# A transformer block on one core: a written order for its first input tiles, and the edges of its attention

## The chip, the cores and the metric

The kernel runs on one core of a Trainium2 chip. The metric is the device time of one execution in microseconds (us). The time of the kernel before is 2206.74 us, the median of three runs (2206.45 to 2209.09).

A core has a matrix engine (TensorE, PE in the profile, with PEld for its weight loads), a vector engine (VectorE, DVE), a scalar engine (ScalarE, ACT), GpSimd (POOL) and a sync engine (SP) that issues most DMA transfers. The engines run side by side, each takes its own instructions in order, and semaphores hold them to one another. Matrix products are written to PSUM, which has eight banks of 128x512 f32; SBUF is the working memory.

## The reference, cut to what matters

One block of a diffusion transformer for 512 latent tokens and 256 context tokens, width 2048, in float32:

```python
mod_l = (silu(c) @ w_ada + b_ada)[:, None, :]          # six vectors of 2048
mod_c = (silu(c_ctx) @ w_ada + b_ada)[None, None, :]
h_l = modulate(rms_norm(x, g_mix_norm), sh_a, sc_a)
h_c = modulate(rms_norm(ctx, g_mix_norm), csh_a, csc_a)
qa_l, kva_l, kr_l, cb_l, cc_l, ch_l = split_projection(h_l @ w_in)
qa_c, kva_c, kr_c, ... = split_projection(h_c @ w_in)
k_l, v_l = mla_key_value(kva_l, kr_l, g_kv_a, w_kv_b, rope_lat)
k_c, v_c = mla_key_value(kva_c, kr_c, g_kv_a, w_kv_b, None)
q_l = mla_query(qa_l, g_q_a, w_q_b, rope_lat)           # rms_norm(q_a, g_q_a) @ w_q_b
att_l = block_attention(q_l, [k_l, k_c], [v_l, v_c])    # softmax(q k * 192**-0.5) v, 8 heads
conv_l = short_conv(cb_l, cc_l, ch_l, conv_w, conv_b)
x = x + gt_a * merge_heads(att_l, conv_l, g_mix_out, w_out)
hf_l = modulate(rms_norm(x, g_ffn_norm), sh_f, sc_f)
x = x + gt_f * conv_ffn(hf_l, w_up, ffn_conv_w, ffn_conv_b, w_down)   # 2 x 5504 wide
return rms_norm(x, g_final)
```

## The kernel before

Activations lie transposed: a tile is 128 channels by 512 tokens, and x is 16 such tiles. Every product is made in three passes: both operands are split into a rounded part (hi, type fp32r, a cast on ScalarE) and the rest (lo, a subtraction on VectorE), and `mm3` (lines 169 to 172) multiplies hi by hi, hi by lo and lo by hi into one PSUM bank. `split` and `blocks` (145 to 164) do this for weights, `hilo` (297) for activations. Instructions are put in order by a planner that simulates the program on a timeline; `keep` holds an instruction in the order in which it is written, and `tc.issue_after(ins)` puts the instructions of its block behind `ins` on the same engine.

The stages in order of time:

- **Front** (lines 405 to 416). `silu_rows` loads c, spreads it over the partitions with a product by ones and takes its SiLU into `sv`. The 16 tiles of x are loaded; `add_squares` squares each on ScalarE and adds the squares on VectorE into one running sum. Then `silu_rows` does the same with c_ctx (tile `cc`, into `svc`), the table of small vectors `sm` is loaded, and `rms` sums the squares over the partitions (products with a column of ones, L283), takes the root and the reciprocal (`rsqrt`, 261 and 262) and spreads the result over the partitions (`spread`, L267) into `rl`.
- **Input projection** (524 to 569). Its 16 input tiles are taken in three chunks (`KCH = [2, 4, 10]`), and within a chunk over 31 column tiles of 128, the first six of them row by row (`pf`), the others one by one (`pp`); `evac` copies or adds the bank into `acc`. `prep(j)` makes input tile j: two rows of w_ada of 1 MB each (t = 16 + j and j) are loaded as two halves and multiplied with `sv` on VectorE with a running sum (`dot_v`, L216), and `modulate` (395) scales x by `rl` (398), by scale and shift (401) and splits it. `todo` (518) says after which column which tile is made. `ctx_mods` (481) does the same dots for the context with `svc` (L491) in the third chunk.
- **Attention** (576 to 801). `ctx_tile` projects the context. The loop (772) has 32 steps, eight heads by four blocks of 128 query rows. `softmax` (678) takes the maximum of a row of scores (L683), multiplies it by -SCALE (L684) and takes the exponential (L687); `transposes` (690) turns p by six transposes (L700) and splits it; `attend` multiplies by the values (`po`). `pieces` makes the next pair of heads' q, k and v in the same steps, `fetch` loads their weights. `merge_sum` (718) sums the squares of a pair of heads and raises them to -1/2 on GpSimd (L732); `merge` (735) spreads that by products with the identity (L741). `gn_apply` does the same for the convolution's groups. Meanwhile the later rows of w_ada (t = 32 to 79) are loaded whole (`ada_raw`, tile `ra`) into the same two `raw` buffers as the weights, and multiplied by `late_dot` (L238).
- **Output projection** (886 to 906). Six columns row by row over 16 rows (`of`), eight columns one by one (`whole`, `o`), and the last two in two halves of 256 tokens (`ol`); `residual` adds to x, and squares for the next norm are summed.
- **Upward projection** (1000 to 1122). The first six columns row by row (`uf`), the others, in pairs f, by a scheme of seven products of half matrices; `acts` (933) makes convolution, SiLU and gate of a pair. `first_acts` (1092) holds the three pairs that come from the first six columns.
- **Downward projection** (1173 to 1226) in three groups of columns, and the last norm.

PSUM is handed out from two pools until line 1038: four tiles of one bank (`sml`) and two of two banks (`big`), which `bank` and `first_banks` deal out in turn. The norm's sums, the scores of a step and the pair `ol` are `big` tiles. From line 1039 on there are eight tiles of one bank, in the cyclic order of `BANKS` (36).

SP's queue takes the loads of x, w_in and w_ada in written order up to line 548 (`ordered`).

## Time and profile before

| | |
|---|---|
| median of three runs | 2206.74 us (2206.45 to 2209.09) |
| the profiled execution, its own time | 2206.8 us |
| its span, first to last instruction | 2204.9 us, 34542 instructions |
| mean granted TensorE clock | 0.996 |
| read from HBM, written | 442.73 MB, 20.71 MB |
| DMA queue of SP (hardware_dynamic, q1) | 405.03 MB, 54.1% of 16 engines' span |
| chain of work that ended last, by engine | TensorE 91%, VectorE 4%, DMA 2%, ScalarE 2% |

The profile records one execution. Its times differ from the runs' by the 1.9 us that lie around the span. Busy shares are means over stages with different limits, so the stages have to be read one by one; a row of the table of stages gives the length of a stretch and, for each engine, its busy time and (in brackets) its instructions, then the granted clock of TensorE as a share of full speed, the busy share of the DMA engines and what they moved. In a line of a group stand the code line, engine and operation, what it writes and reads, the shape and count, then the busy time and the mean length of one in ns, and the idle time of the engine just before these instructions with what ended it. Matmuls are pipelined, so a record of one is longer than its distance to the next.

### The profile page before, as it was taken

The page shows a single profiled execution, that of the slowest core. Times are in us where ns is not written, and L with a number is a line of the kernel's source. Part 1 is how long each engine was busy: PE and PEld are TensorE (multiplying, and loading weights), DVE is VectorE, ACT ScalarE, POOL GpSimd, SP SyncE. Part 2 cuts the span into 40 slices and gives each one's busy share as a digit, 9 for nine tenths or more (in the row PEclk, how much of TensorE's full clock was granted, in tenths as well). Part 3 has the DMA queues.
Part 4 walks back from the last instruction along what each step waited for, and adds up shares of the span by engine and source line. Part 5 has one row for each costly group of instructions (what it writes and reads, how often), then busy time and mean ns, then how long its engine had stood idle before and what let it go on. Part 6 is the DMA issues. An engine that isn't in the chain of part 4 may idle for free.

```text
span 2204.9 us, 34542 instructions
## 1 busy us (share of the span) xinstructions
PE 2149.2 (97%) x13346; PEld 1914.2 (87%) x13346; DVE 1599.0 (73%) x2493; ACT 1010.5 (46%) x1635; POOL 111.3 (5%) x149
## 2 busy tenths in 40 slices
PE   7899999999999999999999999999999999999998
PEld 4688888878888888899999999999999888888887
DVE  7998887678896848777777777777777873633544
ACT  5523333544452237555554555555554432532444
POOL 0000000000000000011111011111110000000000
PEclk9999999999999999999999999999999999999999
DMA  8989884434469925577777777777776995753462
GB/s 331 344 276 334 275 279 150 144 120 149 158 235 358 331 86 172 132 196 201 204 194 195 201 205 195 194 201 201 201 193 200 350 345 159 247 164 92 160 210 88
DMA packets 144264, 466.75 MB, mean 212 GB/s; under 512 B 16290, under 2 KB 20642, under 8 KB 138082
## 3 DMA queue, kind: packets, MB, share of 16 engines
q1 hardware_dynamic: 125652, 405.03, 54.1%
q0 software_dynamic: 16272, 57.42, 12.8%
q8 instruction: 104, 1.70, 0.3%
q10 hardware_dynamic: 2176, 2.10, 0.3%
q14 instruction: 60, 0.49, 0.1%
HBM read 442.73 MB, written 20.71 MB: 210 GB/s over the span
## 4 chain that ended last, share of the span: by engine, by line
PE 91%; DVE 4%; DMA 2%; ACT 2%; issue 1%; SPq 0%; POOL 0%; DVEq 0%; ACTq 0%
PE d L170 7%; PE d L172 7%; PE d L171 7%; PE pp L170 4%; PE pp L172 4%; PE pp L171 4%; PE o L172 1%; PE o L171 1%; PE o L170 1%; PE uf L170 1%; PE uf L171 1%; PE uf L172 1%; PE of L172 1%; PE pf L171 1%; PE of L170 1%; PE of L171 1%
## 5 line engine op out<-in xcount | busy, mean ns | idle before, releaser
L997 POOL DMA_DIRECT2D u_s<-in_w_up x80 | 68.1, 851 | 416.3 <-DMA u_s<-in_w_up 353.4
L153 ACT CAST w_0h<-rw 128x512 fp32r<-128x512 f32 (+1 forms) x63 | 38.5, 618 | 107.3 <-PE pp L171 65.7
L216 DVE SCALAR_TENSOR_TENSOR ada<-ada,sv 128x1024 f32<-128x1024 f32 x64 | 77.4, 1217 | 4.6 <-DMA ada<-in_w_ada 4.6
L491 DVE SCALAR_TENSOR_TENSOR ada<-ada,svc 128x1024 f32<-128x1024 f32 x64 | 75.9, 1218 | 2.0 <-DMA ada<-in_w_ada 1.8
L238 DVE SCALAR_TENSOR_TENSOR ra<-ra,sv 128x1024 f32<-128x1024 f32 x50 | 59.4, 1216 | 0.0
L154 DVE TENSOR_TENSOR w_0l<-rw,w_0h 128x512 fp32r<-128x512 f32 (+1 forms) x63 | 42.4, 680 | 21.8 <-ACT w_0h L153 21.8
L238 DVE SCALAR_TENSOR_TENSOR ada<-ada,sv 128x1024 f32<-128x1024 f32 x46 | 55.7, 1218 | 2.6 <-DMA ada<-in_w_ada 2.6
L1108 DVE TENSOR_TENSOR u<-u,u 128x1024 f32<-128x1024 f32 x40 | 49.0, 1225 | 1.3
L1107 DVE TENSOR_TENSOR u<-u,u_s 128x1024 f32<-128x1024 f32 x40 | 48.7, 1217 | 0.0
L939 POOL DMA_DIRECT2D y_d<-a x43 | 24.7, 576 | 386.2 <-DVE a L938 376.7
L732 POOL TENSOR_TENSOR gr<-gr,half 128x8 f32<-128x8 f32 x4 | 8.3, 2084 | 641.4 <-DVE mx L684 505.3
L238 DVE SCALAR_TENSOR_TENSOR adl<-adl,sv 128x1024 f32<-128x1024 f32 x32 | 38.8, 1218 | 0.2 <-DMA adl<-in_w_ada 0.2
L683 DVE TENSOR_REDUCE mx<-s 128x1 f32<-128x768 f32 x32 | 30.4, 951 | 8.4 <-PE s L673 8.4
L704 DVE TENSOR_TENSOR ptl<-t,pth 128x384 fp32r<-128x384 f32 x64 | 33.2, 548 | 4.2 <-ACT pth L703 4.2
L502 DVE TENSOR_TENSOR acc<-acc,pp 128x512 f32<-128x512 f32 x50 | 33.9, 678 | 1.9 <-PE pp L172 1.8
L703 ACT CAST pth<-t 128x384 fp32r<-128x384 f32 x64 | 28.5, 488 | 14.3 <-PE t L700 14.1
L936 ACT ACTIVATE g<-g 128x512 f32<-128x512 f32 x43 | 27.2, 633 | 12.1 <-DVE g L930 12.1
L928 ACT ACTIVATE g<-cg,sm 128x512 f32<-128x512 f32 x40 | 32.5, 813 | 0.0
L687 ACT ACTIVATE p<-s,mx 128x768 f32<-128x768 f32 x32 | 29.3, 915 | 6.8 <-DVE mx L684 6.6
L928 ACT ACTIVATE a<-ca,sm 128x512 f32<-128x512 f32 x40 | 32.1, 802 | 0.0
L700 PE MATMUL t<-io,p 128*128 128x128 f32 x192 | 27.5, 274 | 3.7 <-ACT p L687 2.4
L929 DVE SCALAR_TENSOR_TENSOR g<-cg,sm,g 128x511 f32<-128x511 f32 x40 | 29.8, 745 | 0.0
(15580 smaller groups left out, 8734.8 us busy)
## 6 DMA issues: line engine op xcount, KB each, us to landing
ada<-in_w_ada SPq DMA_DIRECT2D x174, 512.0 KB, 6.0
u<-in_w_up SPq DMA_DIRECT2D x120, 512.0 KB, 8.3
u_s<-in_w_up SPq DMA_DIRECT2D x80, 512.0 KB, 4.1
u_s<-in_w_up POOLq DMA_DIRECT2D x80, 512.0 KB, 9.5
d<-in_w_dn SPq DMA_DIRECT2D x86, 384.0 KB, 3.8
y<-y_d SPq DMA_DIRECT2D x129, 256.0 KB, 4.5
ra<-in_w_ada SPq DMA_DIRECT2D x25, 1024.0 KB, 4.8
adl<-in_w_ada SPq DMA_DIRECT2D x32, 512.0 KB, 6.0
```

The costliest lines, as they stand in the source:

```text
L153: A.copy(out=hi[:, :n], in_=raw[:, a:a + n])
L154: V.tensor_tensor(out=lo[:, :n], in0=raw[:, a:a + n], in1=hi[:, :n].bitcast(F32), op=ALU.subtract)
L170: PE.matmul(ps, w[0], x[0], start=first, stop=False, skip_group_check=on_top)
L171: PE.matmul(ps, w[0], x[1], start=False, stop=False, skip_group_check=on_top)
L172: PE.matmul(ps, w[1], x[0], start=False, stop=last, skip_group_check=on_top)
L216: V.scalar_tensor_tensor(out=r, in0=r, scalar=1.0, in1=vec[:, i * 1024:(i + 1) * 1024], op0=ALU.mult, op1=ALU.mult, accum_out=col[:, i:i + 1])
L238: keep(V.scalar_tensor_tensor(out=r, in0=r, scalar=1.0, in1=svs[i], op0=ALU.mult, op1=ALU.mult, accum_out=lc[:, t % 4:t % 4 + 1] if i else ...
L491: keep(V.scalar_tensor_tensor(out=raw[q], in0=raw[q], scalar=1.0, in1=svc[:, q * 1024:(q + 1) * 1024], op0=ALU.mult, op1=ALU.mult, accum_o ...
L928: A.activation(u, src, AF.Identity, bias=s("fb", m), scale=s("fw", 86 + m))
L997: G_.dma_start(r[-1], src[more], accum_op=ALU.add)
L1107: V.tensor_tensor(out=a11, in0=a11, in1=s1, op=ALU.add)
L1108: V.tensor_tensor(out=a12, in0=a12, in1=a11, op=ALU.add)
```

## The change

It has several parts.

1. **Front.** `sm` is loaded ahead of x. The order of ScalarE and VectorE is written out (`pinned`, `pin`) from the start to the second input tile. The squares are added up in groups of five, each group is summed on TensorE when it is complete, and the last tile of x is a group of its own. The rows t = 16, 0, 17 and 1 of w_ada are loaded and multiplied in quarters (`ada_quarters`, `dot_quarter`), and weights of the first two tiles are split at written places (`low`). After that the casts of weights are held behind the second tile's cast (`gate`) until the eighth column of the first chunk. c_ctx is no longer loaded here: at the second chunk one DMA spreads it over the partitions and one activation takes its SiLU.
2. **Spreading.** `spread` and `merge` transpose a broadcast column instead of multiplying it by the identity.
3. **Attention.** -SCALE is folded into `g_q`; `softmax` takes the minimum, and the exponential has scale -1. `q_nope(1, 0)` is made ahead of the loop, `merge` comes one step later, weights are fetched and late tiles loaded at other steps, the last four `gn_apply` run inside the loop, and the exponential's table is asked for early.
4. **End of attention.** The eight single banks begin here. Four of the 16 rows of the output projection's first six columns (`OUT_EARLY`) stand ahead of `merge(3)`.
5. **Banks.** `ol`, the norm's sums and `uf` are single banks, and `BANKS` has another order.
6. **First activations.** One of the three pairs is taken in the middle of the first turn, one at its end, one at the end of the next.

The diff, cut to its core:

```diff
-BANKS = [0, 1, 7, 4, 5, 6, 2, 3]
+BANKS = [7, 6, 2, 3, 4, 5, 1, 0]
+OUT_EARLY = 4
...
+    def pin(ins):
+        if pinned[0]:
+            keep(ins)
+        return ins
...
-        A.copy(out=hi[:, :n], in_=raw[:, a:a + n])
-        V.tensor_tensor(out=lo[:, :n], in0=raw[:, a:a + n], in1=hi[:, :n].bitcast(F32), op=ALU.subtract)
+        with tc.issue_after(gate[0]) if gate else ExitStack():
+            pin(A.copy(out=hi[:, :n], in_=raw[:, a:a + n]))
+        if not pinned[0]:
+            V.tensor_tensor(out=lo[:, :n], in0=raw[:, a:a + n], in1=hi[:, :n].bitcast(F32), op=ALU.subtract)
+            return hi, lo
+        lows.append((lo, hi, raw, a, n))
...
     def spread(pb, r):
         for g in range(r.shape[1]):
-            PE.matmul(pb[:, g * P:(g + 1) * P], bc(r[:, g:g + 1], P), ident, start=True, stop=True)
+            PE.transpose(pb[:, g * P:(g + 1) * P], bc(r[:, g:g + 1], P), ident)
...
+        def dot_quarter(t):
+            q, col = quarters[t]
+            i = 4 - len(q)
+            r = q.pop(0)
+            pin(V.scalar_tensor_tensor(out=r, in0=r, scalar=1.0, in1=sv[:, i * T:(i + 1) * T], op0=ALU.mult, op1=ALU.mult, accum_out=col[:, i:i + 1]))
+            if i == 3:
+                pin(V.tensor_tensor(out=col[:, :2], in0=col[:, :2], in1=col[:, 2:], op=ALU.add))
+                total(col, t, mod[:, t:t + 1])
...
-        silu_rows(c, sv, "c")
...
-        silu_rows(c_ctx, svc, "cc")
-        fetch_to(sm, small)
-        rms([ssq], D, T, rl)
+        pinned[0] = True
+        A.activation(tiny(1, "silu"), eps, AF.Silu)
+        silus = silu_rows(c, sv, "c")
+        next(silus)
+        fetch_to(sm, small)
+        xs = []
+        def squares():
+            for j in range(NK):
+                xs.append(t2([P, T], F32, f"xr{j}"))
+                fetch_to(xs[j], xt[:, j * T:(j + 1) * T])
+                if j == NK - 1:
+                    quarters[16] = ada_quarters(16)
+                ssq = add_squares(ssq if j % 5 else None, xs[j], T, f"xs{j}")
+                if j in (1, 3, 5):
+                    next(silus)
+                if j == NK - 1:
+                    dot_quarter(16)
+                    dot_quarter(16)
+                if j % 5 == 4 or j == NK - 1:
+                    yield ssq
+        quarters = {}
+        rms(squares(), D, T, rl, 4)
+        dot_quarter(16)
+        dot_quarter(16)
+        first_raw = load(w_in[:, :2 * G * P], 2 * G * P, "rf00")
+        quarters[0] = ada_quarters(0)
+        quarters[17] = ada_quarters(17)
+        quarters[1] = ada_quarters(1)
+        first_w = blocks(first_raw, 8, "wf00")
+        normed(0)
+        for _ in range(4):
+            dot_quarter(0)
+        modulate(0, 2)
+        first_w += blocks(first_raw, 4, "wf08", 8)
+        low()
+        for t in (17, 1):
+            for _ in range(4):
+                dot_quarter(t)
+        normed(1)
+        modulate(1)
+        pinned[0] = False
+        gate.append(last_hi[0])
...
+                fetch_to(svc, c_ctx.to_broadcast([P, D]))
+                A.activation(svc, svc, AF.Silu)
...
-            mx = tiny(1, f"mx{hd}{tt}")
-            V.tensor_reduce(mx, ss[:, :768], axis=AX.X, op=ALU.max)
-            V.tensor_scalar(mx, mx, scalar1=-SCALE, scalar2=None, op0=ALU.mult)
+            mn = tiny(1, f"mn{hd}{tt}")
+            V.tensor_reduce(mn, ss[:, :768], axis=AX.X, op=ALU.min)
...
+        fetch(1, 0)
+        late_load(ada_raw)
         for f, i in ((k_ctx, 0), (k_ctx, 1), (values, 2)):
             f(0, i)
...
+        q_nope(1, 0)
+        fetch(1, 1)
...
-            elif n % 8 == 1 and n > 1:
+            if n % 8 == 2 and n > 8:
                 merge(n // 8 - 1)
             late_dot(1)
-            if n % 4 != 3:
+            if n > 24 and n % 2:
+                deque(late_bg[4 + (n - 25) // 2], 0)
+            at = n % 8
+            if at == 0 and n and n < 24:
+                fetch(pr + 1, 1)
+            if pr < 3 and n:
+                f, p_, i = pieces(pr + 1)[at]
+                f(p_, i)
+            if at < 2 and n < 24:
+                fetch(pr + 1, 2 + at)
+            elif at >= 2 and n < 29:
                 late_load(ada_raw)
+                if at == 6 and n < 16:
+                    fetch(pr + 2, 0)
+            if n in (29, 30):
+                k = 2 * (n - 29)
+                out_raw[k] = load(w_out_first[k // 2], 2 * G * P, f"ofr{k}")
             pump(2)
+        ph_ps.close()
+        p8 = ctx.enter_context(tc.tile_pool(name="p8", bufs=1, space=PSUM, reuse_waits="tile"))
...
         merge_sum(3)
-        for g in late_bg[4:]:
-            deque(g, 0)
+        pss = [bank_of(g, f"of{g}") for g in range(G)]
+        mix = []
+        for k in range(OUT_EARLY):
+            if k % 2 == 0:
+                w = row_weights(w_out_first, k, "of", raw=out_raw[k])
+            out_row(k, w)
         merge(3)
...
-    b = big("ol")
-    pso = [b[:, :512], b[:, 512:]]
+    pso = [sml("ol0"), sml("ol1")]
...
-    pss = first_banks("uf")
+    pss = [bank_of(i, f"uf{g}") for g, i in enumerate((2, 3, 4, 5, 1, 0))]
...
-        while first_acts:
+        if first_acts and f == G // 2:
             acts(*first_acts.pop(0))
```

More of the change, by code (lines that the diff above doesn't have):

```diff
@@ L389, in mods, with normed @@
             ada(j)
+        def normed(j):
+            keep(V.tensor_tensor(out=xs[j], in0=xs[j], in1=rl, op=ALU.mult))
         def prep(j):
@@ L573, in block_kernel, with half_of, row, row_weights @@
         del spare["w"]
+    HS = [slice(0, T // 2), slice(T // 2, T)]
+    def half_of(w, h):
+        return tuple(z[:, HS[h]] for z in w)
+    def row(pss, w, x, k, cols=slice(0, T)):
+        for g in range(G):
+            mm3(pss[g][:, cols], w[g], tuple(z[:, cols] for z in x), k == 0 and cols.start == 0, k == NK - 1)
+    def row_weights(src, k, nm, held=False, raw=None):
+        raw = load(src[k // 2], 2 * G * P, f"{nm}r{k}") if raw is None else raw
+        if held:
+            r = []
+            for b in range(0, 2 * G, 4):
+                w = hilo(raw[:, b * P:(b + 4) * P], 4 * P, f"{nm}w{k}_{b}")
+                r += [part(w, q) for q in range(4)]
+        else:
+            r = blocks(raw, 2 * G, f"{nm}w{k}")
+        return r[:G], r[G:]
     mixa = [None] * NH
@@ L739, in merge @@
                 pb_ = sml(f"gb{hd}")
-                for g in range(4):
-                    PE.matmul(pb_[:, g * P:(g + 1) * P], bc(r[:, i * 4 + g:i * 4 + g + 1], P), ident, start=True, stop=True)
+                spread(pb_, r[:, 4 * i:4 * i + 4])
                 o = oo[hd]
@@ L1036, in block_kernel @@
         t_sums(j)
-    ph_ps.close()
-    p8 = ctx.enter_context(tc.tile_pool(name="p8", bufs=1, space=PSUM, reuse_waits="tile"))
-    banks = deque(BANKS)
-    def bank_of(i, nm):
-        return p8.tile([P, 512], F32, tag=f"s{i}", bufs=1, name=nm)
-    def bank8(nm):
-        banks.rotate(-1)
-        return bank_of(banks[-1], nm)
-    for i in range(8):
-        bank_of(i, f"bank{i}")
+    bank8 = in_turn(BANKS)
     one_bank[0] = bank8
```

138 lines of the change are left out of this document (73 added, 65 removed).

## The prediction

> **What bounds the kernel now.** I read the busy line first, then a table of the engines' busy time by stage, then TensorE's waits over the whole run, its waits inside the attention loop, and last the chain of waits up to the first real product.
>
> ```profile
> PE 2149.2 (97%) x13346; PEld 1914.2 (87%) x13346; DVE 1599.0 (73%) x2493; ACT 1010.5 (46%) x1635; POOL 111.3 (5%) x149
> ```
>
> TensorE is occupied for 97% of the span, so no edit can win more than what lies in its gaps, in stages where it only looks busy, and in products that are not needed. The table of stages (length, then PE, PEld, DVE, ACT and POOL busy, granted clock, DMA share, GB/s) says where that is.
>
> ```profile
> 0.00:30.24 30.24, 18.55 (x32) 8.25 (x32) 19.50 (x36) 21.11 (x35) 0.20 (x4) 1.00 0.95 357
> 30.24:88.00 57.76, 49.91 (x194) 37.43 (x195) 51.06 (x104) 30.01 (x55) 0.00 (x0) 1.00 0.89 327
> 88.00:160.00 72.00, 72.00 (x311) 57.91 (x310) 71.04 (x135) 26.93 (x44) 0.00 (x0) 1.00 0.84 296
> ...
> 436.00:625.00 189.00, 178.69 (x1193) 160.25 (x1192) 152.66 (x298) 89.23 (x193) 5.79 (x3) 1.00 0.40 140
> 625.00:652.00 27.00, 22.38 (x147) 19.26 (x146) 26.51 (x53) 17.02 (x35) 2.55 (x1) 0.94 0.72 264
> ...
> 800.00:838.00 38.00, 34.78 (x257) 33.28 (x256) 22.91 (x49) 20.79 (x40) 2.70 (x5) 0.96 0.43 146
> ...
> 895.00:925.00 30.00, 25.68 (x174) 24.14 (x173) 24.85 (x31) 15.46 (x21) 2.53 (x4) 0.94 0.44 114
> ```
>
> Five places lose time: the 30.24 us before the first product of the input projection (its 32 matmuls are row broadcasts and norm sums, none of the projection); the first two input tiles to 88 us, 7.9 us idle; the attention loop, 10.3 us idle; its end at 625 to 652, 4.6 us idle with VectorE at 98%; and two joints at 800 and 895, 3.2 and 4.3 us idle. At the last three the clock is also below 1: 0.06 x 27 = 1.6 us, 0.04 x 38 = 1.5 us, 0.06 x 30 = 1.8 us.
>
> TensorE's waits (who waited for whom: us in total, times, longest) name the causes, the first fence over the whole run, the second for 436 to 625 us.
>
> ```profile
> PE pp L170 <- ACT acc L500: 6.9, 6, 1.7
> PE u3c L170 <- ACT u3q5h L921: 4.3, 1, 4.3
> ...
> PE po L171 <- DVE ptl L704: 2.4, 1, 2.4
> ...
> PE ol L170 <- ACT o151w512h L153: 0.7, 1, 0.7
> PE ol L170 <- ACT o141w512h L153: 0.7, 1, 0.7
> ```
>
> ```profile
> PE s L669 <- ACT p L687: 3.4, 3, 1.5
> PE t L700 <- ACT p L687: 2.1, 1, 2.1
> PE pq L172 <- DVE wq12l L154: 1.3, 1, 1.3
> ```
>
> The chain of waits to the first product (start, length, what):
>
> ```profile
> 15.64 7.17 PE cc L376 x8
> 22.83 0.60 ACT svc L377
> 23.45 1.28 ACT L261
> 24.74 0.27 ACT rr L261
> 25.04 0.19 DVE rr L262
> 25.27 2.09 PE rs L267 x8
> 27.38 0.59 ACT rl L290
> 28.00 0.70 DVE xr L398
> 28.73 0.82 ACT xr L401
> 29.57 0.63 ACT h0h L300
> ```
>
> Here the context's row (`cc`, eight matmuls) stands in TensorE's and ScalarE's order ahead of the norm's sums (`rs`), although x's squares are done long before. The last square, the first product with the second input tile, and the dots with the modulation weights:
>
> ```profile
> 16.43 0.63 ACT L317 ACTIVATE xs<-xr 128x512 f32<-128x512 f32 x1 [0.17 <-DVE xs0t L318]
> 38.50 0.73 PE L170 MATMUL pf<-h1h,wf_4h 128*128 128x512 f32 x2 [0.33 <-ACT h1h L300]
> L216 DVE SCALAR_TENSOR_TENSOR ada<-ada,sv 128x1024 f32<-128x1024 f32 x64 | 77.4, 1217 | 4.6 <-DMA ada<-in_w_ada 4.6
> ...
> L238 DVE SCALAR_TENSOR_TENSOR ra<-ra,sv 128x1024 f32<-128x1024 f32 x50 | 59.4, 1216 | 0.0
> ```
>
> **The change part by part.**
>
> **1. The front.** The `cc` products leave it. The last square ends at 16.43 + 0.63 = 17.06. The table `sm` (128x550 f32, 0.28 MB) now goes ahead of x; at the 357 GB/s of the first stage that is 0.8 us of later x, so I put the last square at 17.2. Then, with the durations of the chain: sums 1.9 (as from the end of `cc` at 22.81 to the root at 24.74), root 0.27, reciprocal 0.19, the spreading half of 2.09, copy 0.59, about 0.2 between them: rl at 21.4 instead of 27.97. The root's table load (1.28) runs beside the sums. From there the modulation vectors bind: by then 4.19 (x) + 0.28 + 1.05 (w_ada tile 16) + 0.79 (first weights) + 1.05 (tile 0) = 7.4 MB must have landed, 20.7 us at 357 GB/s; as that mean holds an almost empty start I take 23. After it a quarter dot (half of 1.217), two short sums (0.3), scale 0.16, 0.82 and 0.63: the first product at about 25.7 against 30.24. Tiles 17 and 1 add 2.1 MB, 5.9 us at that rate, so the second tile's product comes at about 32 against 38.50. The 18 products of the first tile fill the time between. SP's new order puts all of this in its queue before the next weights; those are queued behind it and are needed only after the 36 products of the six first columns.
>
> The gate holds the first weight casts behind the second tile's cast on ScalarE; behind them wait the column products, and the same 36 products cover them. Quarter dots ahead of the reciprocal on VectorE need only the first half of tile 16, which lands before the sums end. Front: **-6.5**, bounds -3.8 (only the first product's gain lasts) and -8. To 88 us VectorE is the fuller engine (51.06 of 57.76) and part of its idle time is a wait for `ada`; the queue is now ahead by two tiles, so some of the 6.9 us that TensorE waits for evacuation should go: **-2**, bounds 0 and -5.
>
> The context's row is now one DMA of 1 MB and one SiLU of 128x2048 on ScalarE during 88 to 160, where ScalarE is busy 26.93 of 72. By the four `svc` activations of 0.60 it is 2.4 us plus two table loads of 1.28: 5 us beside a full TensorE, cost nothing; if ScalarE stood for the DMA with nothing cast ahead, up to 5.
>
> **2. Spreading by transposes.** `spread` (and `merge`, L741) now transposes a broadcast column instead of multiplying it by the identity. These are the lines of the three forms:
>
> ```profile
> L700 PE MATMUL t<-io,p 128*128 128x128 f32 x192 | 27.5, 274 | 3.7 <-ACT p L687 2.4 <-ACT o L716 0.9
> ...
> L267 PE MATMUL gb<-io,gn 128*128 128x128 f32 x64 | 8.5, 287 | 0.0
> L741 PE MATMUL gb<-io,gr 128*128 128x128 f32 x64 | 8.0, 278 | 1.0 <-POOL gr L732 1.0
> ```
>
> The 8 groups of four columns in `gn` and the 8 in `merge` leave 64 records each: two passes a column, 8.0/64 = 0.125 us each. The 192 transposes of the loop leave one record each, 27.5/192 = 0.143 us. So a column costs 0.143 instead of 0.25: 0.107 saved. Beside those 64 columns there are 20 outside the front (norms): 84 x 0.107 = 9.0. A few stand where TensorE waits anyway: **-7.5**, bounds 0 and -9.
> The Trainium skill (TensorE: Matmul & The Clock Gate, Terms) says that the transpose mode makes FP32 four times faster. The trace has one record against two, a factor of 1.75 by the two quotients; by the page a column would fall to 0.06 and this term to about -14.
>
> **3. The attention loop.** The scale goes into g_q, so one 128x1 operation between the row extreme and the exponential leaves (32 times), the next pair's weights are fetched one or more steps earlier, `q_nope(1, 0)` stands before the loop, and the merge one step later than the sum it needs. Late tiles go from 25 to 22 and are kept out of most steps that fetch weights. The waits for `p` (3.4 + 2.1) and for the weights (1.3 and smaller) are what this addresses; I take half of the 10.3 us: **-5**, bounds +1 and -10.
>
> **4. Its end.** Four rows of the output projection (72 products of 128x512; the 311 of the full stage 88 to 160 take 72 us, so 0.23 each: 16.7 us) now stand between the last head and `merge(3)`. They cover the POOL power (2.55 busy in that stage) and the wait for `ptl`, which came because VectorE was full: the last three steps load no late tile, so six or more dots of 1.217 leave it. 4.6 idle + 1.6 clock: **-5**, bounds -1.5 and -6.2.
>
> **5. PSUM in eight single banks.** The two `ol` waits come after evacuations from the other half of one two-bank tile; with two tiles they go: **-1.4**, bounds 0 and -3.2 (the whole idle time at 800).
>
> **6. First activations one by one.** At 895 the three `acts` stood in one burst ahead of the cast `u3q5h`; now one is there, one at the end of that turn, one in the next. **-4.5**, bounds -1 and -6.1 (4.3 + 1.8).
> The Trainium skill (TensorE: Matmul & The Clock Gate, The HAM clock gate) lets the clock fall after an idle window of about 3.4 us. By it, a remaining wait of 2 us here would keep the full clock. The rows speak against it: at 800 to 838 the clock is 0.96 though the whole stage idles 3.2 us in several pieces, so a short rest may still cost its 1.5.
>
> BANKS in another order is a relabelling in the steady turns; it only fits the banks of the first columns to the turn that frees them.
>
> **The sum**, against the profiled execution of 2206.8 us (span 2204.9 and 1.9 around it; the median of three is 2206.74): 6.5 + 2 + 7.5 + 5 + 5 + 1.4 + 4.5 = 31.9, so 2206.8 - 31.9 = 2174.9; I say **2175**.
>
> **The rivals.**
> - **The front's gain is lost before 88.** VectorE has four prep steps of about 9 us (four dots of 1.217, two casts' remainders and three splits of about 0.69, small ones) against 25 columns for TensorE; if weights or dots come late, 8.5 us goes. For: VectorE is 88% busy there. Against: it also waits 4.6 us for `ada`. 2183.
> - **The loop only trades waits,** and its end with it, as VectorE (152.66 of 189) stays the partner: terms 3 and 4 fall to -2: 2183.
> - **The transposes cost what the two passes did,** as the broadcast operand is read with stride zero: 2182. That is the case of the change not doing what it says.
> - **More goes than I count:** terms 1, 3, 5 and 6 near their good ends: 31.9 + 4.5 + 5 + 1.8 + 1.6 = 45, so 2162. The skill's factor of four would add to this case.
> - **Slower: the two raw buffers.** In the loop, 22 late tiles share two buffers with 16 weight fetches on SP's one queue. A dot whose tile has not landed stands at VectorE's head, and the maxima and `ptl` behind it, so TensorE stops. A step lasts about 6 us (189/32) and a load of 1 MB takes 2.9 us at 357 GB/s, so it needs a load issued over 3 us late; from 1.5 us a tile on, 22 tiles eat the 32 us won; at 2.2 us it is 48: 2223. Against: these dots idle 0.0 now, in the group `ra` quoted above.
>
> **How the numbers follow.** Forecast 0.45; front lost 0.15; loop lost 0.14; transposes 0.05; more 0.11; slower 0.05; two or three of the losses together, 2191 to 2199, 0.05. One measurement can tell about 0.2% from no change, 4.4 us, so faster means under 2202.3: 0.91; within 0.04; slower 0.05. The range takes in "more" to a little below, and two losses at once: 2158 to 2193.
>
> **What would show it.** Right: no `cc` matmul, `rl` near 21.5, the first projection product near 26 and the second tile near 32; 88 records fewer in the spreading; clock 1.00 at the end of the loop with `of` products before the last `gb`; no `ol` wait; no 4 us wait of `u3c`. Wrong: the stage from the first product to the last of `h1` longer than 57.8 us; `ra` dots with idle time before them; spreading columns of 0.25 us; idle TensorE in the loop of 10 us as before. What would overturn it is a new wait that repeats, in the loop or in the 40 turns of the upward products.

## The result and the profile after

The changed kernel takes **2189.34 us** (median of four, 2188.44 to 2193.24), the kernel before, measured beside it, 2207.91 us (2206.45 to 2211.14): a ratio of 0.9917, 95% interval 0.9900 to 0.9934. Two later pairs gave 0.9905 [0.9885, 0.9925] and 0.9901 [0.9885, 0.9916]. The profiled execution of the changed kernel took 2188.99 us, its span is 2187.2 us. So it is 18.6 us faster by the first pair of medians where 31.9 were forecast; faster, and inside the range, but with less than two thirds of the gain.

The busy line of the page, and then the table of stages for the stretches that answer to the five places of the prediction (the stretch and its length, then PE, PEld, DVE, ACT and POOL busy with their instructions, granted clock, DMA share, GB/s). The first two rows meet at the first product, and the last two are shifted with their joints. The rows from 440 and from 629 us have the length of their rows before, but the loop is 15 us shorter now, so the first reaches to its end and the second lies behind it. Two rows are therefore added: the inside of the loop to 611, and 611 to 640, its end, which answers to the row 625 to 652 before.

```profile
PE 2138.3 (98%) x13274; PEld 1914.9 (88%) x13274; DVE 1593.5 (73%) x2479; ACT 1012.1 (46%) x1635; POOL 112.9 (5%) x149
```

```profile
0.00:28.92 28.92, 15.58 (x45) 10.25 (x45) 16.28 (x41) 17.68 (x31) 0.20 (x4) 1.00 0.96 345
28.92:88.00 59.08, 49.02 (x190) 37.38 (x191) 50.97 (x111) 29.97 (x55) 0.00 (x0) 0.97 0.88 327
440.00:629.00 189.00, 182.66 (x1227) 164.98 (x1225) 162.04 (x291) 100.33 (x218) 7.54 (x3) 0.99 0.42 148
629.00:656.00 27.00, 27.00 (x128) 22.36 (x128) 24.39 (x45) 9.79 (x19) 2.55 (x1) 0.99 0.86 309
784.00:822.00 38.00, 36.06 (x275) 35.02 (x274) 23.41 (x50) 21.33 (x41) 2.70 (x5) 0.96 0.45 148
878.00:908.00 30.00, 30.00 (x230) 28.96 (x229) 23.40 (x28) 17.18 (x23) 2.75 (x5) 1.00 0.54 133
```

```profile
440.00:611.00 171.00, 168.94 (x1134) 152.41 (x1132) 144.04 (x256) 88.01 (x190) 7.54 (x3) 1.00 0.42 148
611.00:640.00 29.00, 24.71 (x146) 21.85 (x147) 29.00 (x54) 19.20 (x41) 0.00 (x0) 0.94 0.57 200
```

Read against the rows before: the inside of the loop is now close to full (2.1 us idle), and so is the joint at 878 (4.3 us idle became 0.0, with the clock at 1.00). The joint at 784 idles 1.9 us instead of 3.2, at the same clock of 0.96. The end of the loop is nearly as it was: 4.3 us idle of 29 with VectorE full and the clock at 0.94, where 4.6 of 27 were idle at 0.94. The first row of the projection is no better: 10.1 us idle of 59.08, where 7.9 of 57.76 were, and the clock dips to 0.97.

TensorE's waits over the whole run name these two places, the first tiles and the end of the loop, and one more in the third chunk of the projection (`w_0l`) (who waited for whom: us in total, times, longest):

```profile
PE pp L193 <- ACT acc L589: 6.6, 6, 2.4
PE pf L193 <- ACT h0h L329: 5.9, 1, 5.9
PE pf L193 <- ACT h1h L329: 3.4, 1, 3.4
...
PE pp L195 <- DVE w_0l L168: 2.6, 2, 2.3
PE po L194 <- DVE ptl L819: 2.6, 1, 2.6
```

The waits for `u3q5h`, for `gr` and for the two `ol` evacuations are gone; `acc`, which was to shrink, stands at 6.6 after 6.9; the wait for `ptl` is still there; and 3.4 us for the second tile's `h1h` are new (0.3 before).

A second table sets the landmarks of the program beside each other in five traces: the two of the kernel before (the first is the one of the prediction; the second was taken later) and three of the changed one. They are the starts and ends of products, taken from the traces; each row is the time from the landmark above it, in us.

| from the landmark above to | before | before, again | changed | again | third |
|---|---|---|---|---|---|
| first product of the projection | 30.24 | 29.84 | 28.92 | 28.68 | 29.47 |
| end of the projection (last with tile 15) | 373.85 | 373.05 | 378.64 | 376.32 | 378.73 |
| first scores | 32.15 | 32.43 | 32.13 | 32.13 | 32.09 |
| last `po` of the attention | 204.26 | 206.97 | 189.15 | 187.79 | 188.04 |
| last `of` | 74.04 | 73.73 | 69.89 | 69.57 | 69.58 |
| first `ol` | 89.36 | 89.37 | 89.06 | 89.06 | 89.06 |
| last `ol` | 26.13 | 26.06 | 23.80 | 23.80 | 23.80 |
| first `u3a` | 71.84 | 70.40 | 71.78 | 70.50 | 70.50 |
| first `u4a` | 17.57 | 18.70 | 11.53 | 11.53 | 11.53 |
| first `u42a` (38 turns) | 757.57 | 766.08 | 766.08 | 766.08 | 766.08 |
| end | 527.92 | 526.10 | 526.21 | 527.32 | 526.70 |

Three things are to be seen. The attention and its end won 15 + 4 us, the last `ol` 2 and the first turn 6. The projection takes 2.5 to 5 us longer; with its start 0.8 to 1.6 us earlier it ends 0.9 to 4.1 us later than in the first trace of before, where 8.5 us were to be won. And the steady turns of the upward products, which the change does not touch but for the numbers of the banks, took 757.57 us in the first trace of before and 766.08 in its second and in every other trace: the profile on which the prediction was built had these turns 8.5 us shorter than any later one.

### The profile page after: what moved, and what is told of

Its sections match the earlier page's. It is cut to its first block, busy times and chain, and to the rows that moved or that the text cites. A ratio compares the mean times of both kernels' runs of the same rounds, so it can differ in the third digit from the quotient of the medians.

```text
span 2187.2 us, 34388 instructions
## 1 busy us (share of the span) xinstructions
PE 2138.3 (98%) x13274; PEld 1914.9 (88%) x13274; DVE 1593.5 (73%) x2479; ACT 1012.1 (46%) x1635; POOL 112.9 (5%) x149
## 4 chain that ended last, share of the span: by engine, by line
PE 92%; DVE 4%; DMA 2%; ACT 1%; issue 1%; SPq 0%; DVEq 0%; ACTq 0%
PE d L193 7%; PE d L195 7%; PE d L194 7%; PE pp L193 4%; PE pp L195 3%; PE pp L194 3%; PE o L193 1%; PE o L195 1%; PE o L194 1%; PE uf L193 1%; PE uf L194 1%; PE uf L195 1%; PE of L193 1%; PE of L194 1%; PE of L195 1%; PE pf L195 1%
## 5 line engine op out<-in xcount | busy, mean ns | idle before, releaser
L263 DVE SCALAR_TENSOR_TENSOR ra<-ra,sv 128x1024 f32<-128x1024 f32 x44 | 52.5, 1221 | 1.1 <-DMA ra<-in_w_ada 1.0
L847 POOL TENSOR_TENSOR gr<-gr,half 128x8 f32<-128x8 f32 x4 | 10.1, 2522 | 632.8 <-DVE gr L846 540.9
L799 DVE TENSOR_REDUCE mn<-s 128x1 f32<-128x768 f32 x32 | 30.5, 955 | 5.1 <-PE s L788 4.9
L802 ACT ACTIVATE p<-s,mn 128x768 f32<-128x768 f32 x32 | 29.3, 916 | 1.6 <-DVE mn L799 1.3
L1065 DVE SCALAR_TENSOR_TENSOR a<-ca,sm,a 128x511 f32<-128x511 f32 x40 | 29.8, 746 | 0.0
```

Of the source, the lines that this page charges most:

```text
L263: keep(V.scalar_tensor_tensor(out=r, in0=r, scalar=1.0, in1=svs[i], op0=ALU.mult, op1=ALU.mult, accum_out=lc[:, t % 4:t % 4 + 1] if i else ...
```

## The experiments

Three questions were open: where the front's 8.5 us had gone, whether the steady turns were slower because of the new bank order, and which parts of the change carry the gain that there is. Each kernel is the changed one with the edit shown. Times are medians with their lowest and highest; the ratio is to the kernel before of the same measurement (2211.69 us for the first four, 2215.89 for the next four, 2210.78 for the last four). The next four (the front in another order without its gate, only the row moved, no rows ahead, the burst) ran on another chip than the other eight, without the changed kernel beside them, so they are compared by their ratios.

### The changed kernel and the kernel before, again

> The changed kernel once more, unaltered. In its first trace a product in the upward turns comes every 120.0 ns (20.16 us a turn of 168 products), in that of the kernel before every 118.7 ns (19.94 us). Theory 'program': the pace belongs to the program, so 20.16 us a turn again and a time of 2188 to 2193 us. Rival 'execution': the pace is drawn anew with each execution; then 19.94 can come up, with a time about 8 us lower.

> The kernel before once more, unaltered. Theory 'program': 19.94 us a turn again. Rival 'execution': 20.16 can come up, with a time about 8 us higher than 2207.

The changed kernel took 2190.25 us (2184.55 to 2192.72), 0.9905 [0.9885, 0.9925]; the kernel before 2214.57 in its single execution. The landmarks stand above. The stretch from 1100 to 1500 us, which is full in all traces, shows the pace; the three rows are of before, of before again and of the changed kernel:

```profile
1100.00:1500.00 400.00, 400.00 (x3373) 400.00 (x3373) 303.24 (x343) 210.00 (x281) 45.52 (x60) 1.00 0.74 199
```

```profile
1100.00:1500.00 400.00, 400.00 (x3335) 400.00 (x3335) 299.38 (x337) 207.39 (x278) 45.45 (x60) 1.00 0.74 196
```

```profile
1100.00:1500.00 400.00, 400.00 (x3336) 400.00 (x3335) 299.08 (x337) 208.90 (x280) 44.81 (x59) 1.00 0.73 196
```

3373 products in 400 us are one in 118.6 ns, 3335 one in 119.9 ns, at a granted clock of 1.00 in both and with no idle time. The same program had both paces, so this is not the change's doing. The chip of the first trace is not on record, so whether the execution or the chip sets the pace is open.

### The bank order

```diff
-BANKS = [7, 6, 2, 3, 4, 5, 1, 0]
+BANKS = [5, 6, 2, 3, 0, 1, 7, 4]
-    pss = [bank_of(i, f"uf{g}") for g, i in enumerate((2, 3, 4, 5, 1, 0))]
+    pss = [bank_of(i, f"uf{g}") for g, i in enumerate((2, 3, 0, 1, 7, 4))]
```

> The changed kernel with the old cyclic order of the eight PSUM banks in the upward turns (5, 6, 2, 3, 0, 1, 7, 4 instead of 7, 6, 2, 3, 4, 5, 1, 0, with the first columns' banks placed to match). Theory 'banks': the new neighbourhood of banks sets the slower pace; then a turn takes 19.94 us and the whole about 8 us less than the changed kernel. Rival 'a relabelling', as predicted: the order of the banks does nothing in the steady turns; then 20.16 us a turn and the same time within 2 us, and the pace has its cause elsewhere in the program.

2189.17 us (2183.85 to 2192.50), 0.9901 [0.9881, 0.9922]: the changed kernel's ratio. The turns take 20.16 us each in both, as in before's second trace (19.94 in its first), and the wait for `u3q5h` stays away. In the steady turns the order is a relabelling, as the prediction had it.

### The old front behind the new rest

Here everything up to the second input tile is as before, with c_ctx's row ahead of the norm.

```diff
-        pinned[0] = True
-        A.activation(tiny(1, "silu"), eps, AF.Silu)
-        silus = silu_rows(c, sv, "c")
...
+        for _ in silu_rows(c, sv, "c"):
+            pass
...
+            ssq = add_squares(ssq, xs[j], T, f"xs{j}")
+        for _ in silu_rows(c_ctx, svc, "cc"):
+            pass
+        fetch_to(sm, small)
+        rms([ssq], D, T, rl)
...
-                fetch_to(svc, c_ctx.to_broadcast([P, D]))
-                A.activation(svc, svc, AF.Silu)
```

> The changed kernel with the front of the kernel before (squares in one running sum, c_ctx's row in the front, whole tiles of w_ada, no written order, no gate); everything else as changed. Theory: the new front costs time, as the changed kernel stands 3.5 us behind at the end of the input projection (404.1 against 407.6 us); so this is 3 to 5 us faster than the changed kernel, with the second input tile's first product at about 38.5 us and the projection's end at about 404. Rival, as predicted: the new front wins 8 us, and what is lost later has another cause; then this is slower than the changed kernel by 2 us or more.

> The changed kernel with the whole old front, a second time and in more rounds. If the old front is really faster behind the same rest, as the first run had it, its time is again 4 to 6 us under the changed kernel's of the same call, with the intervals of the two ratios apart. If that was the scatter of the executions (clock dips and pace), the two medians are within 3 us and the intervals overlap.

2184.08 us (2181.28 to 2186.25), 0.9876 [0.9858, 0.9895], and the second time 2184.02 (2180.63 to 2187.61), 0.9879 [0.9861, 0.9897], beside a changed kernel of 2188.78 (2187.34 to 2190.53), 0.9901 [0.9885, 0.9916]. The two medians of that measurement are 4.8 us apart and the two intervals still overlap, so neither branch of the second expectation came whole; but all of it points one way: eight executions with the old front lie between 2180.63 and 2187.61, the twelve of the changed kernel between 2184.55 and 2193.24. **The new front does not win 8.5 us; by the medians it costs about 5**, the row's new place counted in. By the ratio one other kernel is as good as the change with the old front: the front in another order without its gate (0.9877, below).

The traces place only a part of that. From the first product to the end of the projection the two old fronts take 376.21 and 375.28 us, the three changed ones 378.64, 376.32 and 378.73. As the old fronts begin later, their projections end at 407.11 and 404.32 us, the changed ones at 407.56, 405.00 and 408.20. Both old fronts lose clock early in the projection, as the row of the second one shows:

```profile
28.92:90.00 61.08, 53.45 (x198) 39.97 (x199) 51.98 (x105) 30.48 (x57) 0.00 (x0) 0.94 0.88 322
```

0.06 x 61.08 is 3.7 us. The eight executions have a granted clock of 0.997 on the average, the twelve of 0.995; 0.002 of 2186 us is 4.4, about the difference in time. At the same recorded clock, 0.996 or 0.997 (a step of 0.001 is 2.2 us), the two kernels lie close together: five executions with the old front take 2183.54 to 2187.61 us, three of the changed kernel 2184.55 to 2188.99. So most of the 5 us goes with the clock. In which stage the executions without a trace lost it was not recorded, and that the new front's order is what lowers it is not shown.

### Why the new front is late: the chain of waits

This is about the forecast: behind the same rest the old front's first product comes no earlier (30.91 and 29.04 us, 28.92 here). The chain of the changed kernel's trace (start, length, what), from the last adds of the third group of squares to the first tile:

```profile
17.05 0.70 DVE xs10t L347
...
17.80 3.58 PE rs L312 x16
...
21.41 0.27 ACT rr L289
...
21.70 0.19 DVE rr L291
...
21.93 1.13 PE rs L296 x4
...
23.09 0.59 ACT rl L319
...
23.70 0.69 DVE xr L437
24.40 2.46 DVE aq L422 x8
...
27.40 0.82 ACT xr L450
...
28.25 0.63 ACT h0h L329
```

No DMA stands in it. The last add of the third group of squares ends at 17.75, half a microsecond after the last square (16.61 + 0.63 = 17.24, on ScalarE), so the sums of two groups, 16 products of 0.22 us, came after it instead of those of one. The four quarter dots of tile 0 were written behind the scaling by `rl`, so their 2.46 us began at 24.40, though `sv` was there and the last of their quarters had landed at 23.85. After the first tile come eight dots of tiles 17 and 1, one after the other, on VectorE (30.11 to 35.53 us), while TensorE has nothing left of the first tile from 34.8 on: the gate holds the casts of further weights.

### The same front in another order

All four quarters of tile 16 ahead of the reciprocal, the dots of tile 0 ahead of its scaling; first without the gate, then with it.

```diff
                 if j == NK - 1:
-                    dot_quarter(16)
-                    dot_quarter(16)
+                    for _ in range(4):
+                        dot_quarter(16)
...
         rms(squares(), D, T, rl, 4)
-        dot_quarter(16)
-        dot_quarter(16)
...
-        normed(0)
         for _ in range(4):
             dot_quarter(0)
+        normed(0)
...
-        gate.append(last_hi[0])
```

> The changed kernel with its written front in another order: all four quarter dots of tile 16 ahead of the reciprocal, the four of tile 0 ahead of the norm's product with x (normed), and no gate on the weight casts. Theory 'written order': in the changed kernel VectorE stands idle 2.7 us for the reciprocal and then makes four dots (2.5 us) between rl and the first tile, and eight more before the second, with TensorE idle 3.6 us; so the first product comes about 2 us earlier (near 26.7 us), the second tile's near 36, and the whole is 2 to 4 us faster than the changed kernel. Rival 'transfers': the weights' landing binds, as predicted; then the dots of tile 0 wait for their DMA in the new place and the first product stays at 28.7 to 29.

> The changed kernel with two moves in VectorE's written order of the front, the gate kept: all four quarter dots of tile 16 ahead of the reciprocal, and the dots of tile 0 ahead of the scaling of tile 0. Theory (VectorE's written order is the bound of the front, and without the gate the planner put casts and other dots ahead of the second tile): the first projection product at about 27.5 us as without the gate, and the second tile's at 36 to 37.5 instead of 40.6; the end of the projection no later than in the changed kernel, and the time 0 to 3 us shorter than the changed kernel's. Rival (the front's gain is lost before 90 us whatever the order, to w_ada's tiles): the second tile's product comes early too, but the first product with the third tile is again at 85 us or later and the time is that of the changed kernel.

Without the gate: 2185.94 us (2182.97 to 2187.22), 0.9877 [0.9848, 0.9906]; first product at 27.46, but the second tile's only at 40.60, as casts and dots of later tiles went ahead of it. With the gate: 2187.27 us (2183.82 to 2190.98), 0.9900 [0.9883, 0.9916]; first product at 27.23, second tile at 36.52, third at 80.10 (85.81 in the changed kernel). So VectorE's written order was indeed what held the front, and mending it moves the first three tiles forward by 1.7, 1.7 and 5.7 us against the changed kernel's first trace. The rival "transfers" was right in one point: in the new place the dots of tile 0 do wait for their transfers. Without the gate the first, third and fourth of its quarters landed at 22.03, 23.39 and 24.06 us, and their dots began at 22.05, 23.41 and 24.09. Once the order is mended, the bytes bind.

But the time is that of the changed kernel (2188.78 beside it). A part of the 5.7 us goes in the third chunk of the same trace: the stage, and TensorE's only wait between 180 and 404 us.

```profile
210.00:240.00 30.00, 25.62 (x109) 20.59 (x108) 30.00 (x56) 9.30 (x16) 0.00 (x0) 0.94 0.89 310
```

```profile
PE pp L195 <- DVE w_0l L168: 4.4, 1, 4.4
```

VectorE is busy for 30.00 of 30.00 us, mostly with sums into `acc` and the dots for the context, and the low half of a weight, which TensorE needs, stands in its order behind them. In the first trace of before this wait is 0.8 us, in the changed kernel 2.3. The projection ended at 403.21 us, 0.9 before the first trace of before and 1.8 to 5.0 before the three of the changed kernel. So the earlier start is paid back in part at the next place where VectorE is full. The traced execution is also the fastest of its five (2183.82), and where the other four lost the rest was not recorded.

### Only the row moved

The old front without the `cc` products, and c_ctx's row at the second chunk as in the change.

```diff
         for j in range(NK):
             xs.append(t2([P, T], F32, f"xr{j}"))
             fetch_to(xs[j], xt[:, j * T:(j + 1) * T])
             ssq = add_squares(ssq, xs[j], T, f"xs{j}")
-        for _ in silu_rows(c_ctx, svc, "cc"):
-            pass
         fetch_to(sm, small)
         rms([ssq], D, T, rl)
...
+                fetch_to(svc, c_ctx.to_broadcast([P, D]))
+                A.activation(svc, svc, AF.Silu)
```

> The changed kernel with the front of the kernel before, but without the context's row in it (it is loaded by one DMA and activated in the second chunk, as in the change). Alone, this part should bring rl from 28 to about 22.5 us, as the norm's sums no longer stand behind the products of the row. Theory 'order, not row': the row is the one good part of the new front, so this is 2 to 4 us faster than the kernel with the whole old front (2184 us), with the first product at 25 to 27 us. Rival 'VectorE pays': the dots of tiles 16 and 0 ran under the row, and with it gone they come out as a wait; then the first product stays near 30 us and the time within 1 us of the old front's. Rival 'late row costs': the one activation of 128x2048 stands in ScalarE's way in the second chunk; then TensorE waits there and this is slower than the old front.

2187.90 us (2185.88 to 2190.36), 0.9888 [0.9858, 0.9918]. Taking out the `cc` products alone brings the first product to 27.75 us, earlier than the whole written order does (28.92), and the third tile's to 83.42. Yet the ratio is not under those of the old front with the row in place (0.9876 and 0.9879). In the trace, 322.27 us pass from the third tile's first product to the end of the projection, against 318.28 and 319.13 with the row ahead of the norm. TensorE's waits for the third chunk in this kernel, and the row's activation in the changed one (start, length), are

```profile
PE pp L195 <- DVE w_0l L168: 2.3, 1, 2.3
```

```profile
95.53 1.92 ACT L637 ACTIVATE svc<-svc 128x2048 f32<-128x2048 f32 x1
```

The same wait is 2.3 to 2.4 us long in seven of the ten traces with the late row (0.3, 3.3 and 4.4 in the others), and 0.5 to 1.6 in the four with the early row. The granted clock from 210 to 240 us is 0.94 in seven of the ten, this kernel's among them, and 1.00 in all four, as here with the old front:

```profile
210.00:240.00 30.00, 28.44 (x128) 22.93 (x127) 29.39 (x54) 9.57 (x18) 0.00 (x0) 1.00 0.86 304
```

From the third tile's first product to the end of the projection the ten take 319.0 to 325.4 us, the four 318.3 to 319.2. That speaks for a cost of the late row of some microseconds, on a step that was booked at nothing; the ratios' intervals overlap, and why the wait is longer with it was not found, so it is not settled.

### The spreading by products

```diff
-            PE.transpose(pb[:, g * P:(g + 1) * P], bc(r[:, g:g + 1], P), ident)
+            PE.matmul(pb[:, g * P:(g + 1) * P], bc(r[:, g:g + 1], P), ident, start=True, stop=True)
```

> The changed kernel, with the spreading (norms and merge) again as a product of the broadcast column with the identity; nothing else. Theory (each transposed column costs half of a product's column, 0.13 us against 0.25, and most columns stand on TensorE's path): the records of these lines double (64 for each pair in the norms and in the merge), their busy time goes from about 4 to 8 us in each, and the time is 7 to 10 us longer than the changed kernel's, about 2197. Rival (the spreading lies mostly where TensorE waits for something else, so that it is cheap either way): records double all the same, but the time is longer by less than 4 us, about 2191, and TensorE's idle time in 611 to 640 and at the joints falls by what its busy time gains.

2199.47 us (2193.92 to 2203.15), 0.9947 [0.9927, 0.9967], against 0.9901 [0.9885, 0.9916] for the changed kernel beside it: 10.7 us slower, the largest loss among the parts that were undone one at a time. The groups of the spreading (busy, mean ns, idle before), in the changed kernel and in this one:

```profile
L296 PE MATMUL gb<-io,gn 128*128 128x128 f32 x32 | 4.3, 273 | 0.0
...
L296 PE MATMUL gb<-io,gr 128*128 128x128 f32 x32 | 4.1, 272 | 0.0
```

```profile
L296 PE MATMUL gb<-io,gn 128*128 128x128 f32 x64 | 8.3, 278 | 1.2 <-DVE ptl L819 1.2
L296 PE MATMUL gb<-io,gr 128*128 128x128 f32 x64 | 7.8, 275 | 0.0
```

One record a column instead of two, 0.13 us instead of 0.25. Inside the loop much of it is cover: with the dearer form TensorE's idle time between the first scores and the last `po` falls from 6.4 to 2.5 us, and the stretch is only 1.8 us longer (189.85 after 188.04). From there to the last `of` it is 4.6 longer (74.17 after 69.58): 1.0 is the eight more records, and the rest a wait of 1.8 for `gq` and a clock of 0.98. 3.9 us more lie in the projection (382.65 after 378.73), where the edit adds only ten records, 1.2 us. So the trace places some 6 of the 10.7 us where most of the spreading stands.

### No rows ahead of the last merge, and the burst put back

```diff
-OUT_EARLY = 4
+OUT_EARLY = 0
...
-            w = row_weights(w_out_first, k, "of")
+            w = row_weights(w_out_first, k, "of", raw=out_raw.get(k))
```

> The changed kernel with OUT_EARLY at 0: no row of the output projection ahead of the last merge, everything else as changed. Theory: the four rows cover GpSimd's power and the spreading, so without them the stretch from the last product with values (po) to the end of the projection's first six columns is 3 to 5 us longer than the changed kernel's 69.9 us. Rival: VectorE is full there (29.0 of 29.0 us) and sets the end of the loop with or without the rows; then the stretch changes by under 1 us.

2188.83 us (2187.78 to 2192.39), 0.9897 [0.9863, 0.9932]: no difference. From the last `po` to the last `of` 69.79 us pass, 69.89 with the rows ahead. The row of the end of the loop is nearly the same, here the changed kernel's and then this one's:

```profile
611.00:640.00 29.00, 24.71 (x146) 21.85 (x147) 29.00 (x54) 19.20 (x41) 0.00 (x0) 0.94 0.57 200
```

```profile
611.00:640.00 29.00, 24.58 (x154) 21.21 (x153) 29.00 (x55) 19.41 (x42) 0.00 (x0) 1.00 0.61 217
```

What is won at the end came from elsewhere. Between the last `po` and the last `of` these records of the spreading are left in before and in the changed kernel:

```profile
L267 PE MATMUL gb<-io,gn 128*128 128x128 f32 x24 | 3.0, 276 | 0.0
L741 PE MATMUL gb<-io,gr 128*128 128x128 f32 x16 | 2.0, 281 | 1.0 <-POOL gr L732 1.0
```

```profile
L296 PE MATMUL gb<-io,gr 128*128 128x128 f32 x8 | 1.0, 272 | 0.0
```

5.0 us of records and a wait of 1.0 became 1.0 and none: the convolution's groups moved into the loop (part 3) and the cheaper spreading (part 2). That is read from the records, not tried by itself.

The burst of first activations, in which all three pairs come at one place again:

```diff
-        if first_acts and f == G // 2:
+        while first_acts:
             acts(*first_acts.pop(0))
```

> The changed kernel with the three first activations in one burst again, as before (while for if). Theory: the burst was what held the first turn: 4 to 6 us slower in the turn from u3 to u4 (11.5 us in the changed kernel, 17.6 before), with TensorE waiting for u3c. Rival: the new bank order alone removed that wait; then no difference in that turn.

2190.23 us (2188.60 to 2191.58), 0.9898 [0.9869, 0.9927]: no difference. The turn from `u3a` to `u4a` takes 11.53 us with the burst as without, and the row of the joint is full, as it is with the pairs one by one:

```profile
878.00:908.00 30.00, 30.00 (x228) 28.91 (x227) 26.18 (x34) 18.71 (x26) 3.43 (x5) 1.00 0.56 143
```

So the 6 us of that turn do not come from taking the activations apart. It stands at 11.53 in every kernel whose first six columns lie in single banks of their own, with both bank orders; in before some of them share a tile of two banks, and the pools change behind them. That the tiles are the cause is argued from this, not tried by itself.

## The prediction, point by point

- **The front, -6.5 and -2: this is the step that failed.** The last square was sized rightly (17.2 forecast, 17.24 in the trace), but behind it the prediction wrote "From there the modulation vectors bind", and took 23 us from the bytes to be landed. The last quarter of tile 0 did land at 23.85, near that, but the dots show no wait for their data: VectorE's own order bound. The sum over 16 products (3.58 us where 1.9 was booked, for one group of squares) made `rl` 23.7 instead of 21.4, and the four dots of tile 0 (2.46 us where a quarter dot and two short sums stood) came behind it: the first product at 28.92 instead of 25.7. For the second tile the eight dots of tiles 17 and 1 were counted as bytes only, not as VectorE's time: 38.21 instead of 32. Instead of 8.5 us earlier the projection ended 3.5 us later by the first traces, and with the old front the kernel is 5 us faster by the medians. The rival "the front's gain is lost before 88" was right in that no gain was left there, with the two first tiles already late by VectorE's order; where a gain was made, in the front in another order, it lasted past 88 us and was lost in part in the third chunk. The bound of -3.8, said to be the first product's gain alone, does not follow from the figures beside it: 30.24 - 25.7 is 4.5.
- **The row, 0.** Its price on ScalarE is 3.2 us (table 1.28, activation 1.92) instead of 5, beside a full TensorE. What it does in the third chunk was not looked at; by the stretches above two to four microseconds are possible.
- **Spreading, -7.5: right in cause, a little small.** 0.13 us a column instead of 0.25 (0.143 was taken), 176 records became 88, as forecast, and the kernel is 10.7 us slower when it is undone, above the bound of -9, though the trace places only some 6 of them there; the two ratios' intervals do not overlap. The factor is two: the four of the Trainium skill (TensorE: Matmul & The Clock Gate, Terms) is not what these rows show.
- **The loop, -5: right, and too small.** 204.26 us became 189.15 (188 in the two others). TensorE's idle time from the first scores to the last `po` fell from 13.7 to 6.3, and the spreading inside it is 12.6 us of product distances in before and 7.2 after. The bound of -10 for the idle time held; the rest is work, with the spreading of part 2 in it. The rival of the two raw buffers did not come: the dots `ra` wait 1.1 us in all. Part 3 was not undone by itself, so which of its edits emptied the waits is not shown.
- **Its end, -5: 4.1 us came, behind the last `po` and for another reason.** What the term was to remove is still there: 4.3 us idle at a clock of 0.94 with VectorE busy for 29.00 of 29.00 us, and 2.6 us of wait for `ptl`. The rows ahead of the merge make no difference.
- **Single banks, -1.4:** 2.3 by the `ol` stage (26.13 to 23.80), within the bounds.
- **First activations, -4.5:** 6.0 in that turn, the bound of -6.1; but the named cause, the burst, is not it.
- **The pace:** the profile of before held the upward turns at 118.6 ns a product, and 757.57 us for 38 of them. No other trace has it. Of the 31.9 us forecast against that profile, 8.5 could not come; the front is another 12.0 (+3.5 instead of -8.5); against them stand 4.1 that the attention, `ol` and the first turn won beyond their terms (1.7 + 0.9 + 1.5), and about 2 in stretches without a term (1.7 of it after the last turn). 8.5 + 12.0 - 4.1 - 2 is about 14, the difference between 31.9 and the 17.8 us by which the span fell. Against before's second trace the change wins 25.5 us (2212.72 to 2187.18). How many of the untraced executions of before had which pace is not known.

## What to carry to other kernels

Before crediting a shorter chain of waits, add up what each engine has to do in the written order behind it: here VectorE's own list, dots in a wrong place above all, set the first products, and the transfers bound only when the dots had been moved. A start moved forward can be paid back in the next stage in which the same engine is full, so look for that stage before booking the gain. And undo one part at a time after a change of six: two of the six carried nothing for the reason given, and one, by the medians, cost time inside a kernel that became faster.

## What was not expected of the hardware

The distance of products of 128x256 in a full TensorE at a granted clock of 1.00 was 118.6 ns in one execution and 119.9 in another of the same program, over 38 turns 8.5 us of 766, or 0.4% of the kernel's time. One traced execution out of fourteen had the shorter distance. That is twice the 0.2% that the prediction took as the least that one measurement can tell, so the profile of a single execution does not fix the sum to better than that.

The granted clock in the front does not follow the idle time either: it is 0.94 from 28.92 to 90 us with the old front in the row above, where TensorE idles 7.6 us, 0.97 in the changed kernel, which idles 10.1, and 1.00 in the first row of the projection before, which has the old front too and idles 7.9. At the joint from 784 to 822 us the clock is 0.96 in the row of the changed kernel above, with 1.9 us of idle time; its third trace has 2.0 of idle time there at 1.00:

```profile
784.00:822.00 38.00, 36.01 (x288) 35.15 (x287) 24.69 (x54) 22.82 (x45) 2.71 (x5) 1.00 0.48 157
```

The Trainium skill (TensorE: Matmul & The Clock Gate, The HAM clock gate) ties a fall of the clock to an idle window of about 3.4 us. Here it fell where the whole stretch idles for less, as the prediction suspected, but not in each execution.
